# A decoder block on one core: the opening in written order, with half of its first modulation on TensorE, and the later modulation and squares spread over the projection

## The chip, the cores and the metric

The kernel runs on one core of one Trainium2 chip. The metric is the time of one execution in device microseconds (us). Before the change it is 2672.51 us, the median of 3 runs (2671.59 to 2675.07). A core has TensorE (PE, with its weight load PEld), VectorE (DVE), ScalarE (ACT), GpSimd (POOL) and SyncE (SP), which issues the DMA transfers here. Each engine takes its instructions in order and waits on semaphores of the others.

## The reference

One decoder block over 2048 tokens of width 1024, in float32. A condition vector `c` gives six modulation vectors; an RMS norm scaled and shifted by two of them feeds one wide projection, whose columns go to gated linear attention (4 heads) and to dilated attention (8 heads); an output projection, and a second part with up-projection, causal convolution of width 3, SwiGLU and down-projection follow, each added through a gate.

```
cond = silu(c)
mod = cond @ w_ada + b_ada
sh1, sc1, g1, sh2, sc2, g2 = split(mod, 6)
h = rms_norm(x, norm1_g) * (1 + sc1) + sh1
gq, gk, gv, gr, glr, aq, ak, av = split(h @ w_in)
y_gla = gla_group(gq, gk, gv, log_sigmoid(glr @ gla_w_gate + gla_b_gate) / 16, gr, gla_norm_g)
y_att = dilated_attention_group(rms_norm(aq, q_norm_g), rms_norm(ak, k_norm_g), av)
x = x + g1 * (concat(y_gla, y_att) @ w_out)
h = rms_norm(x, norm2_g) * (1 + sc2) + sh2
u_gate, u_val = split(causal_conv(h @ w_up, conv_w, conv_b), 2)
x = x + g2 * ((silu(u_gate) * u_val) @ w_down)
```

## The kernel before

**Tiles.** The tokens are worked in 4 chunks of 512 (`T`), with features on the 128 partitions; a 1024-wide activation is 8 tiles of 128x512, `k` = 0 to 7. Every matrix product is made in three passes (`mm3`, L282–290): weight and activation are each split into a high part and the rest, and high·high, high·low and low·high are summed in PSUM. A weight block of 128x1024 is loaded by SP (`wraw`, 512 KB), its high part is a ScalarE cast (`whi`, L226), its low part a subtraction on VectorE, or on POOL where `pool=True` (`wlo`, L227). `wraw` has 2 buffers, `whi` and `wlo` 3 each. The weights are prepared in the order of `plan` (two blocks ahead of their use).

**Modulation.** `w_ada` is 48 blocks of 128x1024, one for each 128 values of `mod`. `ada(b)` (L317–335) loads a block, multiplies it by `cond` (the condition on every partition) and sums along the row in one VectorE instruction (L330, a reduce), then adds the bias (L331), and for a scale forms `G` (L335). Blocks 0 to 15 (shift and scale of the first norm) are needed first. The other 32, "late" ones, go through a single buffer (`tag="v4"`): a block's load can be issued only when the reduce of the block before is done.

**Opening.** `run` (L941 on) sets up the condition, loads x of the first chunk, forms its mean square (`norm_stats`, L354–371: 8 squares on ScalarE, adds on VectorE, one matmul with `ones`, L367, then Ln and Exp for 1/root), and then for each `k` emits modulation blocks 8+k and k, for k under 4 one of the first four weight blocks of `w_ch` (`FIRST`, low part on POOL), and `norm_mod1` (L373–386): the product with `G` and 1/root on VectorE (L380, "hmul"), the high part on ScalarE (L382), the low part on VectorE (L384, "hlo"). Then the 4 × 8 products of the first blocks stand, and `consts` (L175–204), whose large load waits until the reduce of k = 6 (`GATE`).

**Projection.** `proj(c)` yields steps in the order of `ORDER0` (first chunk) or `ORDER` (L30/31): g and q blocks from `w_ch` (q blocks take an RMS norm of their own, L403–430, with a square whose mean TensorE forms in L411/412, a Newton step over VectorE and POOL, L350–352, and the staged result L420), V blocks (`av`), W blocks (`wide`, four weight parts each accumulated in four PSUM banks; W1 is evacuated in L458–463 by a Tanh on ScalarE and L461 on VectorE). The four chunks' steps are chained, the 32 late modulation blocks are spread over the first 46 steps by `along`, the statistics of the next chunk stand at step 10 of a chunk in one piece, and its `norm_mod` at W1's end. 27 such steps are emitted before mixing of the first chunk starts beside the rest.

**Order.** The program is emitted in this order, and `TC=dict(schedule_with_timeline_sim=True)` hands it to a scheduler, which places the instructions of each engine anew; the engines then run them in the order it chose.

## Time and profile before

| what | us |
|---|---|
| time, median of 3 runs | 2672.51 |
| lowest and highest run | 2671.59, 2675.07 |
| the profiled execution | 2676.88 |
| its span (first to last instruction) | 2675.1 |
| TensorE busy | 2595.0 (granted clock 0.989 of full on the mean) |
| VectorE, ScalarE, POOL busy | 1891.1, 1273.2, 512.1 |

The profile shows one execution. A row of the timeline has its start and its length in us, engine, line, operation, the tile written and those read, and in brackets how long the engine was idle ahead of it and on what it waited. A row of the groups has count, busy time and mean in ns. A row of the waits has the engine and its line, the engine and line that released it, total, times and longest. L-numbers are lines of the kernel before. Some busy shares of the whole, by 40 slices of 67 us, in tenths:

```profile
PE   5988999999989999999999999999999999999999
DVE  8676784665676866777887777778777766666665
POOL 1142451212221311101231111022211110111110
```

TensorE is at nine tenths in all but the first slices.

### The profile page before, as it was taken

The page shows a single profiled execution, that of the slowest core. Times are in us where ns is not written, and L with a number is a line of the kernel's source. Part 1 is how long each engine was busy: PE and PEld are TensorE (multiplying, and loading weights), DVE is VectorE, ACT ScalarE, POOL GpSimd, SP SyncE. Part 2 cuts the span into 40 slices and gives each one's busy share as a digit, 9 for nine tenths or more (in the row PEclk, how much of TensorE's full clock was granted, in tenths as well). Part 3 has the DMA queues.
Part 4 walks back from the last instruction along what each step waited for, and adds up shares of the span by engine and source line. Part 5 has one row for each costly group of instructions (what it writes and reads, how often), then busy time and mean ns, then how long its engine had stood idle before and what let it go on. Part 6 is the DMA issues. An engine that isn't in the chain of part 4 may idle for free.

```text
span 2675.1 us, 46823 instructions
## 1 busy us (share of the span) xinstructions
PE 2595.0 (97%) x18152; PEld 2122.1 (79%) x18152; DVE 1891.1 (71%) x3756; ACT 1273.2 (48%) x2607; POOL 512.1 (19%) x308
## 2 busy tenths in 40 slices
PE   5988999999989999999999999999999999999999
PEld 3777878888768888888788788878888888788887
DVE  8676784665676866777887777778777766666665
ACT  3445556656645455443545444445455443433332
POOL 1142451212221311101231111022211110111110
PEclk9999999999989999999999999999999999999999
DMA  7868455554552244447434444643344445323222
GB/s 276 295 212 276 160 173 170 186 188 150 173 175 95 93 126 133 124 125 241 135 100 135 133 133 129 197 156 122 104 141 138 140 132 180 131 95 101 97 95 95
DMA packets 192127, 405.09 MB, mean 151 GB/s; under 512 B 19473, under 2 KB 70434, under 8 KB 190626
## 3 DMA queue, kind: packets, MB, share of 16 engines
q1 hardware_dynamic: 191906, 402.11, 46.0%
q8 instruction: 143, 2.34, 0.4%
q14 instruction: 78, 0.64, 0.1%
HBM read 339.12 MB, written 62.91 MB: 150 GB/s over the span
## 4 chain that ended last, share of the span: by engine, by line
PE 77%; DVE 5%; ACT 3%; DMA 2%; issue 1%; POOL 0%; SPq 0%; DVEq 0%; ACTq 0%; POOLq 0%
PE psg L288 22%; PE psg L289 22%; PE psg L290 22%; PE psa L719 2%; PE psa L699 2%; PE psa L821 2%; PE psa L557 1%; DVE wlo L227 1%; ACT whi L226 1%; PE psa L816 1%; PE psa L735 1%; ACT big L709 1%; PE psa L627 0%; PE psa L628 0%; DMA sq<-y 0%
## 5 line engine op out<-in xcount | busy, mean ns | idle before, releaser
L288 PE MATMUL psg<-hhi,whi 128*128 128x512 f32 x2040 | 808.7, 399 | 15.6 <-ACT hhi L382 9.0
L289 PE MATMUL psg<-hlo,whi 128*128 128x512 f32 x2040 | 805.6, 395 | 6.4 <-DVE hlo L384 5.0
L290 PE MATMUL psg<-hhi,wlo 128*128 128x512 f32 x2040 | 803.9, 395 | 0.0
L226 ACT CAST whi<-wraw 128x1024 fp32r<-128x1024 f32 (+1 forms) x391 | 409.6, 1049 | 402.5 <-PE psg L289 307.5
L227 DVE TENSOR_TENSOR wlo<-wraw,whi 128x1024 fp32r<-128x1024 f32 (+1 forms) x300 | 386.1, 1287 | 150.2 <-ACT whi L226 141.4
L227 POOL TENSOR_TENSOR wlo<-wraw,whi 128x1024 fp32r<-128x1024 f32 x91 | 223.7, 2459 | 1340.8 <-ACT whi L226 1138.9
L288 PEld LDWEIGHTS psg<-hhi,whi 128*128 128x128 f32 x2040 | 386.2, 190 | 104.8 <-ACT hhi L382 12.3
L289 PEld LDWEIGHTS psg<-hlo,whi 128*128 128x128 f32 x2040 | 386.4, 189 | 90.3 <-DVE hlo L384 9.8
L290 PEld LDWEIGHTS psg<-hhi,wlo 128*128 128x128 f32 x2040 | 386.5, 189 | 82.3 <-issue 2.0
L288 PE MATMUL psg<-ghi,whi 128*128 128x512 f32 x704 | 280.1, 398 | 0.0
L289 PE MATMUL psg<-glo,whi 128*128 128x512 f32 x704 | 277.1, 394 | 0.0
L290 PE MATMUL psg<-ghi,wlo 128*128 128x512 f32 x704 | 276.3, 392 | 0.0
L933 DVE SCALAR_TENSOR_TENSOR x<-psg,mod,x 128x512 f32<-128x512 f32 x192 | 142.7, 747 | 124.4 <-PE psg L290 120.2
L889 DVE SCALAR_TENSOR_TENSOR y<-psg,conv_w_sb,y 128x511 f32<-128x511 f32 x176 | 130.9, 744 | 88.2 <-ACT y L888 87.9
L288 PE MATMUL psg<-whi,hhi 128*128 128x512 f32 (+2 forms) x512 | 177.5, 353 | 10.5 <-DVE stg L461 7.0
L289 PE MATMUL psg<-wlo,hhi 128*128 128x512 f32 (+2 forms) x512 | 178.7, 349 | 7.2 <-DVE wlo L227 7.2
L290 PE MATMUL psg<-whi,hlo 128*128 128x512 f32 (+2 forms) x512 | 177.3, 349 | 0.0
L288 PEld LDWEIGHTS psg<-ghi,whi 128*128 128x128 f32 x704 | 132.5, 188 | 32.2 <-issue 4.5
L290 PEld LDWEIGHTS psg<-ghi,wlo 128*128 128x128 f32 x704 | 132.5, 188 | 28.4 <-issue 1.0
L289 PEld LDWEIGHTS psg<-glo,whi 128*128 128x128 f32 x704 | 132.7, 188 | 28.1 <-issue 2.1
L709 ACT ACTIVATE big<-big,nm 128x256 f32<-128x256 f32 (+1 forms) x256 | 122.4, 479 | 47.1 <-DVE nm L724 47.1
L581 POOL TENSOR_TENSOR pt<-kt,pt 128x512 f32<-128x512 f32 x56 | 92.4, 1650 | 264.2 <-ACT pt L578 186.5
(199 smaller groups left out, 3617.7 us busy)
## 6 DMA issues: line engine op xcount, KB each, us to landing
wraw<-in_w_up_dram SPq DMA_DIRECT2D x176, 512.0 KB, 3.3
wraw<-in_w_down_dram SPq DMA_DIRECT2D x88, 512.0 KB, 3.3
wraw<-in_w_ch_dram SPq DMA_DIRECT2D x48, 512.0 KB, 4.2
wada<-in_w_ada_dram SPq DMA_DIRECT2D x40, 512.0 KB, 5.0
v<-v SPq DMA_DIRECT2D x68, 256.0 KB, 5.1
wraw<-in_w_tokw_dram SPq DMA_DIRECT2D x32, 512.0 KB, 3.9
wraw<-in_w_out_dram SPq DMA_DIRECT2D x32, 512.0 KB, 4.0
sq<-in_xT_dram SPq DMA_DIRECT2D x48, 256.0 KB, 3.9
```

Source lines behind the costliest of these rows:

```text
L226: nc.scalar.copy(hi[:, :n], raw[:, :n])
L227: (nc.gpsimd if pool else nc.vector).tensor_tensor(lo[:, :n], raw[:, :n], hi[:, :n].bitcast(F32), op=ALU.subtract)
L288: nc.tensor.matmul(ps, wh, hh, start=first and k == 0, stop=False, skip_group_check=shared)
L289: nc.tensor.matmul(ps, wh, hl, start=False, stop=False, skip_group_check=shared)
L290: nc.tensor.matmul(ps, wl, hh, start=False, stop=k == n - 1, skip_group_check=shared)
L581: nc.gpsimd.tensor_tensor(kh, gk, df, op=ALU.mult)
L699: nc.tensor.matmul(at(i, hh, z), q[H[hh], i * P:(i + 1) * P], key(H[hh], i, z), start=True, stop=True, skip_group_check=True)
L709: nc.scalar.activation(t[:, lo:hi], t[:, lo:hi], AF.Exp, bias=nm[:, hh, g, i:i + 1], scale=2.0 ** -(h + 1), accum_out=dn[:, hh, g, i:i + 1])
L719: nc.tensor.transpose(ps[:n, i * P:(i + 1) * P], part(S[hh], i), self.C("id"))
L821: nc.tensor.matmul(out, lhsT, rhs, start=first[hh], stop=False, skip_group_check=True)
L889: nc.vector.scalar_tensor_tensor(y[:, 1:], ps[:, :T - 1], self.cw[:, 1, b:b + 1], y[:, 1:], op0=ALU.mult, op1=ALU.add)
L933: nc.vector.scalar_tensor_tensor(x1, ps, self.mod[:, 40 + cb:41 + cb], x1, op0=ALU.mult, op1=ALU.add)
```

## The change

**The opening** is written out in `begin` (called in place of the opening part of `run`), and its instructions on TensorE, VectorE, ScalarE and SP are pinned: `Pinned` hands each to `keep_in_program_order`, so the scheduler leaves their order. In it

- modulation columns k = 0 to 3 (blocks 0 to 3 and 8 to 11) come from a second layout of the same weights, `w_ada1`, in two groups of 2 MB. `ada_rows` multiplies each by the condition on TensorE: 8 products of a 128x32 operand `crep` (the condition's column repeated 32 times) with 128x512 of weights, into four column groups of one PSUM bank, copied by ScalarE; `ada_sum` brings the result to a column with 4 products of one column each, and VectorE adds the bias and forms `G`. Columns 4 to 7 are still reduced on VectorE;
- 36 matmuls of `ones` by `ones` (128x128), whose result isn't read, stand at the head of TensorE's program;
- the low parts of the four first weight blocks are made on VectorE (on POOL before);
- the first four blocks' products stand between the activations in written order, not behind them.

**Later.** The constants' loads all wait for the last early reduce (`GATE` 7), and the four small instructions on them (`const_ops`) stand after 7 steps of the projection. The late modulation (`ada_late`) is loaded and reduced in halves of 128x512 (256 KB), through one buffer of its own (`tag="th"`), 64 halves spread over 91 emitted steps. The statistics of the next chunk (`stats`) make one square in a step, 10 steps spread over a chunk's, in place of one piece at step 10. As before, 27 steps of the projection stand before the mixing.

```diff
-GATE = 6
+GATE = 7
+WARM = 36
...
+    def ada_rows(self, u, raws):
+        ps = self.pa()
+        for k in range(KD):
+            j = k % 4
+            self.nc.tensor.matmul(ps[32 * j:32 * j + 32], self.crep[:, k], raws[k], start=k < 4, stop=k >= 4, skip_group_check=True)
+        t = self.tmp.tile([P, T], F32, name="sq", bufs=3)
+        self.nc.scalar.copy(t, ps)
+        return t
+
+    def ada_sum(self, u, t):
+        nc = self.nc
+        pm = self.pa()
+        for i in range(4):
+            nc.tensor.matmul(pm[:, i:i + 1], t[:, i * P:(i + 1) * P], self.sel, start=True, stop=True, skip_group_check=True)
...
+    def ada_late(self):
+        nc = self.nc
+        for i in (2, 4, 3, 5):
+            for b in range(8 * i, 8 * i + KD):
+                m = self.mod[:, b:b + 1]
+                for j in range(2):
+                    cols = slice(j * T, (j + 1) * T)
+                    raw = self.up.tile([P, T], F32, name="wada", tag="th", bufs=1)
+                    ld = nc.sync.dma_start(raw, self.A["w_ada"][b][:, cols])
+                    if b == 16 and not j:
+                        self.after(ld)
+                    yield
+                    nc.vector.tensor_tensor_reduce(raw, raw, self.cond[:, cols], 0.5, m if j else 0.0, ALU.mult, ALU.add, m)
+                self.ada_end(b)
...
+    def begin(self):
+        plain = self.nc
+        nc = self.nc = PinnedAll(self.tc)
...
+        idle = self.pa()
+        for _ in range(WARM):
+            nc.tensor.matmul(idle[:, 0:P], self.ones, self.ones, start=True, stop=True)
...
+        whi(0)
+        wlo(0)
...
+        t = self.ada_rows(0, rows[0])
+        ms = self.pa()
+        nc.tensor.matmul(ms, self.ones, acc, start=True, stop=True)
...
+        self.ada_sum(0, t)
+        hmul(0)
+        whi(1)
+        hmul(1)
+        hlo(0)
+        wlo(1)
+        hlo(1)
+        whi(2)
+        wlo(2)
+        mm(0, 0, 1)
+        mm(1, 0, 1)
+        mm(2, 0)
+        t = self.ada_rows(1, rows[1])
+        whi(3)
+        next(late[0], None)
+        wlo(3)
+        mm(2, 1)
+        self.ada_sum(1, t)
+        hmul(2)
+        hmul(3)
+        mm(3, 0, 1)
+        hlo(2)
+        hlo(3)
+        for k in (2, 3):
+            for b in FIRST:
+                mm(b, k)
+        for k in range(4, KD):
...
-        def ahead(g, n, c):
-
-            for i, _ in enumerate(g):
-                if i == n:
-                    rstd[c] = self.norm_stats(src(c))
+        def stats(c):
+            acc = None
+            x = src(c)(0)
+            for k in range(KD):
                 yield
...
+                nx = src(c)(k + 1) if k + 1 < KD else None
+                acc = self.square(acc, x, x)
+                x = nx
+            yield
+            rstd[c] = self.norm_end(acc)
+            yield
+
+        def ahead(c, g):
+            return along(stats(c), 10, g, 14)
+
+        first = proj(0)
+        for _ in range(7):
+            next(first)
+        self.const_ops()
+        gemm = along(self.ada_late(), 64, chain(ahead(1, first), ahead(2, proj(1)), ahead(3, proj(2)), proj(3)), 91)
+        for _ in range(20):
             next(gemm)
```

Three places of VectorE's order, of before and of the change apart. A row has the line, the operation, the tile written and those read, and the size; numbers behind names tell tiles apart. `ISA` is a reduce, followed by a short row that reads its sum out.

The first is the opening, from the first multiplication by `G` on. VectorE before:

```order
L380 SCALAR_TENSOR_TENSOR x_164<-x_164,G1_110,rstd_207 128x512
L330 ISA wada_241,mod_109<-wada_241,cond_93,mod_109 128x512
L330 ISA mod_109 128x1
L335 SCALAR_TENSOR_TENSOR G1_110<-mod_109,norm1_g_sb_95 128x1
L331 TENSOR_TENSOR mod_109<-mod_109,b_ada_sb_99 128x1
L380 SCALAR_TENSOR_TENSOR x_166<-x_166,G1_110,rstd_207 128x512
L384 SCALAR_TENSOR_TENSOR hlo_237<-x_164,mod_109,hhi_235 128x512
L330 ISA wada_262,mod_109<-wada_262,cond_93 128x1024
```

VectorE of the change, where pinned instructions all bear the line of the helper, L143:

```order
L143 TENSOR_TENSOR mod_170<-psa_323,b_ada_sb_151 128x2x2
L143 SCALAR_TENSOR_TENSOR G1_171<-mod_170,norm1_g_sb_149 128x2
L143 SCALAR_TENSOR_TENSOR x_173<-x_173,G1_171,rstd_320 128x512
L143 SCALAR_TENSOR_TENSOR x_175<-x_175,G1_171,rstd_320 128x512
L143 SCALAR_TENSOR_TENSOR hlo_333<-x_173,mod_170,hhi_331 128x512
L143 TENSOR_TENSOR wlo_335<-wraw_199,whi_334 128x1024
L143 SCALAR_TENSOR_TENSOR hlo_340<-x_175,mod_170,hhi_338 128x512
L143 TENSOR_TENSOR wlo_345<-wraw_201,whi_344 128x1024
L143 ISA wada_304,mod_170<-wada_304,cond_147 128x1024
```

The two columns' sums come from PSUM (`psa`) at once, the reduces between the two columns are gone, and the low parts of the weight blocks stand among the activations.

The second is the first wide block W0 of the first chunk, between the low parts of its third and fourth weight part (first and last row). VectorE before:

```order
L227 TENSOR_TENSOR wlo_804<-wraw_801,whi_803 128x1024
L330 ISA wada_795,mod_109<-wada_795,cond_93 128x1024
...
L350 SCALAR_TENSOR_TENSOR nwt_726<-psa_720,eps_103,sq_711 128x512
L365 TENSOR_TENSOR rstd_865<-rstd_865,sq_897 128x512
L330 ISA wada_909,mod_109<-wada_909,cond_93 128x1024
...
L330 ISA wada_943,mod_109<-wada_943,cond_93 128x1024
...
L330 ISA wada_989,mod_109<-wada_989,cond_93 128x1024
L330 ISA mod_109 128x1
L227 TENSOR_TENSOR wlo_834<-wraw_831,whi_833 128x1024
```

VectorE of the change:

```order
L260 TENSOR_TENSOR wlo_846<-wraw_843,whi_845 128x1024
...
L416 ISA wada_996,mod_170<-wada_996,cond_147,mod_170 128x512
...
L416 ISA wada_1112,mod_170<-wada_1112,cond_147 128x512
...
L416 ISA wada_1175,mod_170<-wada_1175,cond_147,mod_170 128x512
...
L416 ISA wada_1235,mod_170<-wada_1235,cond_147 128x512
...
L416 ISA wada_1309,mod_170<-wada_1309,cond_147,mod_170 128x512
...
L416 ISA wada_1372,mod_170<-wada_1372,cond_147 128x512
...
L260 TENSOR_TENSOR wlo_884<-wraw_881,whi_883 128x1024
```

Four whole reduces stood between the two weight parts, and six halves stand there now; `const_ops`' four instructions stand there too (left out).

The third is between the staged results (`stg`) of two neighbouring blocks in the first chunk, q4 and q5 (first and last row). VectorE before:

```order
L420 SCALAR_TENSOR_TENSOR stg_1269<-stg_1270,kgs_473,sq_1263 128x512
L331 TENSOR_TENSOR mod_109<-mod_109,b_ada_sb_99 128x1
L227 TENSOR_TENSOR wlo_1482<-wraw_1479,whi_1481 128x1024
L330 ISA wada_1756,mod_109<-wada_1756,cond_93 128x1024
L330 ISA mod_109 128x1
L350 SCALAR_TENSOR_TENSOR nwt_1339<-psa_1334,eps_103,sq_1325 128x512
L331 TENSOR_TENSOR mod_109<-mod_109,b_ada_sb_99 128x1
L352 SCALAR_TENSOR_TENSOR sq_1325<-nwt_1339,sq_1325 128x512
L330 ISA wada_1790,mod_109<-wada_1790,cond_93 128x1024
L330 ISA mod_109 128x1
L420 SCALAR_TENSOR_TENSOR stg_1331<-stg_1332,kgs_473,sq_1325 128x512
```

VectorE of the change:

```order
L512 SCALAR_TENSOR_TENSOR stg_1284<-stg_1285,kgs_532,sq_1278 128x512
L416 ISA wada_2710,mod_170<-wada_2710,cond_147,mod_170 128x512
...
L260 TENSOR_TENSOR wlo_1503<-wraw_1500,whi_1502 128x1024
L416 ISA wada_2774,mod_170<-wada_2774,cond_147 128x512
L416 ISA mod_170 128x1
L432 SCALAR_TENSOR_TENSOR nwt_1356<-psa_1351,eps_155,sq_1342 128x512
L434 SCALAR_TENSOR_TENSOR sq_1342<-nwt_1356,sq_1342 128x512
L416 ISA wada_2895,mod_170<-wada_2895,cond_147,mod_170 128x512
L416 ISA mod_170 128x1
L512 SCALAR_TENSOR_TENSOR stg_1348<-stg_1349,kgs_532,sq_1342 128x512
```

Two whole reduces stood between the two results; three halves stand there now.

More of the change, by code (lines that the diff above doesn't have):

```diff
@@ L129, in chain, with __init__, __getattr__, call @@
         yield from g
+class Pinned:
+    def __init__(self, tc, eng):
+        self.tc, self.eng = tc, eng
+    def __getattr__(self, name):
+        f = getattr(self.eng, name)
+        def call(*a, **kw):
+            r = f(*a, **kw)
+            self.tc.keep_in_program_order(r)
+            return r
+        return call
+class PinnedAll:
+    def __init__(self, tc):
+        for e in ("tensor", "vector", "scalar", "sync"):
+            setattr(self, e, Pinned(tc, getattr(tc.nc, e)))
 class K:
@@ L204, in consts, with const_ops @@
             self.sb.append(t)
+    def const_ops(self):
+        nc = PinnedAll(self.tc)
+        nc.vector.tensor_scalar(self.qgs, self.C("qsc"), self.qg[:, 0:1], -0.5, op0=ALU.mult, op1=ALU.mult)
+        nc.vector.tensor_scalar(self.kgs, self.kg, -0.5, None, op0=ALU.mult)
+        nc.vector.tensor_scalar(self.gB, self.gB, 0.5, None, op0=ALU.mult)
+        nc.vector.tensor_copy(self.blk, self.C("blk"))
     def scratch(self):
@@ L964, in run @@
-        for b in FIRST:
-            for k in range(KD):
-                self.mm3(done[b], ws[b][k:k + 1], h0[k:k + 1], k == 0, True)
+        done, rstd, h0 = self.begin()
         self.consts()
@@ L985, in proj @@
             yield from self.proj(c, hs.pop(), (lambda: begin(c + 1)) if c < 3 else None, () if c else done)
-        def ahead(g, n, c):
-            for i, _ in enumerate(g):
-                if i == n:
-                    rstd[c] = self.norm_stats(src(c))
+        def stats(c):
+            acc = None
+            x = src(c)(0)
+            for k in range(KD):
                 yield
-        gemm = along(chain(*(self.ada(8 * i + k) for i in (2, 4, 3, 5) for k in range(KD))), 32, chain(ahead(proj(0), 10, 1), ahead(proj(1), 10, 2), ahead(proj(2), 10, 3), proj(3)), 46)
-        for _ in range(27):
+                nx = src(c)(k + 1) if k + 1 < KD else None
[12 more added lines that the diff above has]
+        for _ in range(20):
             next(gemm)
```

189 lines of the change are left out of this document (140 added, 49 removed).

## The prediction

> **What bounds the kernel now.** I read first the page's busy times and slices, then the windows cut at the places where TensorE stops, then the waits of TensorE and VectorE, then the timelines around each stop.
>
> ```profile
> span 2675.1 us, 46823 instructions
> PE 2595.0 (97%) x18152; PEld 2122.1 (79%) x18152; DVE 1891.1 (71%) x3756; ACT 1273.2 (48%) x2607; POOL 512.1 (19%) x308
> 0.00:22.00 22.00, 2.08 (x2) 0.51 (x3) 16.18 (x34) 11.51 (x16) 3.07 (x6) 1.00 0.92 340
> 22.00:43.60 21.60, 14.62 (x30) 9.08 (x31) 21.60 (x47) 5.55 (x7) 5.54 (x3) 1.00 0.79 257
> 43.60:61.50 17.90, 15.66 (x69) 12.22 (x67) 13.89 (x27) 4.26 (x7) 1.90 (x1) 1.00 0.58 201
> 61.50:107.00 45.50, 45.06 (x238) 37.97 (x238) 27.75 (x44) 25.86 (x46) 5.30 (x4) 1.00 0.89 312
> 107.00:112.00 5.00, 0.24 (x2) 0.10 (x1) 4.34 (x6) 0.98 (x2) 1.26 (x1) 0.99 0.26 85
> 178.00:215.00 37.00, 26.66 (x240) 20.24 (x239) 33.88 (x48) 20.27 (x34) 21.76 (x18) 0.82 0.66 215
> 215.00:400.00 185.00, 174.71 (x1509) 143.23 (x1508) 136.02 (x193) 100.60 (x185) 69.42 (x46) 0.97 0.59 198
> 400.00:2675.00 2275.00, 2250.86 (x15748) 1843.83 (x15746) 1594.51 (x3299) 1076.17 (x2274) 387.07 (x218) 0.99 0.43 137
> ```
>
> In the windows the columns are length, then busy time (and instructions) of PE, PEld, DVE, ACT, POOL, then granted clock, DMA share, GB/s. TensorE is busy 97% of the span: 80 us of it are idle. 29 of these lie in the first 61.5 us (22.0 − 2.08, 21.6 − 14.62, 17.9 − 15.66), 4.8 in the one stop at 107, 10.3 in 178–215 (where the clock also falls to 0.82) and 10.3 in 215–400. After 400, where the change moves nothing by hand, 24 us are spread over 2275. Each of the early stops has its releaser:
>
> ```profile
> PE psa L367 <- DVE rstd L365: 14.6, 1, 14.6
> PE psg L288 <- ACT hhi L382: 8.6, 3, 5.4
> PE psa L411 <- ACT sqr L405: 4.6, 1, 4.6
> PE psg L288 <- DVE stg L461: 3.9, 1, 3.9
> DVE wada L330 <- DMA wada<-in_w_ada_dram: 25.8, 18, 3.1
> ```
>
> (Total, times, longest.) The last row is VectorE's, over 62–400: there it stands 25.8 us in 18 waits for modulation weights to land, and TensorE's stops are behind that. The profiled execution took 2676.88 us, 4.37 above the median of 2672.51; I sum against it and subtract that.
>
> **A. The opening: −4 (−6.5 to +1).** Of before:
>
> ```profile
> 9.47 2.59 ACT L360 ACTIVATE sq<-x 128x512 f32<-128x512 f32 x4 [0.30 <-DMA x<-in_xT_dram]
> 14.57 2.08 PE L367 MATMUL psa<-rstd,ones 128*128 128x512 f32 x2 [14.57 <-DVE rstd L365]
> 15.29 1.04 ACT L226 CAST whi<-wraw 128x1024 fp32r<-128x1024 f32 x1 [3.23 <-DMA wraw<-in_w_ch_dram]
> 16.60 3.24 DVE L330 CUSTOM_DVE_ANT_0 wada<-wada,cond 128x1024 f32<-128x1024 f32 x1 [0.48 <-DMA wada<-in_w_ada_dram]
> 20.45 0.74 DVE L380 SCALAR_TENSOR_TENSOR x<-x,G,rstd 128x512 f32<-128x512 f32 x1
> 22.00 1.73 PE L288 MATMUL psg<-hhi,whi 128*128 128x512 f32 x2 [5.35 <-ACT hhi L382]
> 28.75 1.22 DVE L330 CUSTOM_DVE_ANT_0 wada<-wada,cond 128x1024 f32<-128x1024 f32 x1
> 37.23 2.33 DVE L331 TENSOR_TENSOR mod<-mod,b_ada_sb 128x1 f32<-128x1 f32 x1
> 57.72 0.74 DVE L384 SCALAR_TENSOR_TENSOR hlo<-x,mod,hhi 128x512 fp32r<-128x512 f32 x1
> 61.47 0.39 PE L288 MATMUL psg<-whi,hhi 128*128 128x272 f32 x1 [0.81 <-ACT stg L437]
> L384 DVE SCALAR_TENSOR_TENSOR hlo<-x,mod,hhi 128x512 fp32r<-128x512 f32 x8 | 5.9, 743 | 0.7 <-ACT hhi L382 0.7
> ```
>
> The eight early columns k set the end, 61.47. Removed: eight of sixteen reduces (about 1.2 each undisturbed, as at 28.75) and POOL's four lo parts (2.4 to 2.6 each, beside which the reduce at 16.60 took 3.24 and a one-column add at 37.23 2.33). Added: sixteen TensorE products with 32 columns, two ACT copies, and the lo parts on VectorE (1.29 each, L227 of the page's groups).
>
> First product. The last x lands near 11.4 (four squares of 0.65 begin at 9.47). The first cast starts at 15.29, the third 512 KB after it: (15.29 − 11.4)/3 = 1.3 us per 512 KB. Five such loads stand ahead of the first group, so they end at 11.4 + 5 × 1.3 = 17.9. The group (its last pair 1 to 2), the mean's matmul (1 to 2), Ln and Exp (1.3 together) bring the first multiplication by G to T = 22.4, against 20.45: the change begins **2 us later**. An estimate with the half-speed spacing of matmuls gives 23.4, with the full-speed one 21.4.
>
> From T on nothing waits for a load. hmul, hi, whi and lo of two columns and three blocks end 6.9 (full speed) to 9.1 us (half) after T on TensorE; the second group, its copy (0.6) and the cast of the fourth block (1.0) start its lo part at T + 10.5 to 13.4, and I take 12.4. It takes 1.2. Then VectorE's fixed row: the sum's two small ones 0.4; hmul and hlo of two columns 2.7; a reduce with its add 1.35; an hmul 0.7; three rounds of two reduces with adds (2.8), hmul and hlo (0.7 each), 4.2 each; a G more and the last hlo behind ScalarE's hi 1.8: 19.6 in all, to T + 33.2. Some 12 matmuls at 0.23 follow. So the wide V0 block starts at 22.4 + 33.2 + 2.7 = 58.3, taken as 58 (55 to 62) against 61.47: −3.5, and −4 with half of the 0.8 idle ahead of that row, which is a ScalarE copy that will have been free longer. The constants' 710 KB, which held VectorE 2.3 us before 57.45, are behind the last reduce and no longer ahead of an hlo. What is late next is VectorE itself: it is the chain from T on.
>
> **B. The first wide block: +3 (0 to +6).** Before:
>
> ```profile
> 89.59 1.23 DVE L227 TENSOR_TENSOR wlo<-wraw,whi 128x1024 fp32r<-128x1024 f32 x1 [0.25 <-DMA sq<-in_xT_dram]
> 92.90 1.23 DVE L330 CUSTOM_DVE_ANT_0 wada<-wada,cond 128x1024 f32<-128x1024 f32 x1 [2.09 <-DMA wada<-in_w_ada_dram]
> 108.93 1.76 DVE L330 CUSTOM_DVE_ANT_0 wada<-wada,cond 128x1024 f32<-128x1024 f32 x1 [0.66 <-DMA wada<-in_w_ada_dram]
> 111.90 0.79 PE L289 MATMUL psg<-wlo,hhi 128*128 128x512 f32 x1 [4.76 <-DVE wlo L227]
> wada<-in_w_ada_dram SPq DMA_DIRECT2D x40, 512.0 KB, 5.0
> sq<-in_xT_dram SPq DMA_DIRECT2D x48, 256.0 KB, 3.9
> ```
>
> One buffer holds the modulation weight, so a reduce, the issue and the landing follow one another: from 92.90 to 108.93 three rounds of 5.3. Between the lo parts of the third and fourth parts of W0 lay four of these; TensorE waited 4.76 for the fourth lo part. The new order has six halves there. No row has a half-size modulation load; the nearest are the 256 KB loads of x (3.9 median) and the 512 KB one (5.0). With SP stuck behind stores as before a half's round can be hardly shorter than a full one's; with free queues it is 2.5. I take 3.6 (a half's reduce 0.7 plus 2.9, a little under the row of 256 KB since the median holds queued loads). Six give 21.6 against 4 × 5.3 = 21.2. The part is thus about as late as before against its block, which now starts 3.5 earlier; with the stats' squares (0.68 adds, one per step) and const_ops' four (1.0) ahead of it the stop grows from 4.8 to about 8.
>
> **C. The q chain: −5 (−8 to 0).**
>
> ```profile
> 167.24 0.74 DVE L420 SCALAR_TENSOR_TENSOR stg<-stg,kgs,sq 128x512 f32<-128x512 f32 x1
> 172.79 2.15 DVE L330 CUSTOM_DVE_ANT_0 wada<-wada,cond 128x1024 f32<-128x1024 f32 x1 [1.49 <-DMA wada<-in_w_ada_dram]
> 178.44 1.22 DVE L330 CUSTOM_DVE_ANT_0 wada<-wada,cond 128x1024 f32<-128x1024 f32 x1 [0.73 <-DMA wada<-in_w_ada_dram]
> 179.59 0.75 DVE L420 SCALAR_TENSOR_TENSOR stg<-stg,kgs,sq 128x512 f32<-128x512 f32 x1
> 183.16 0.50 PE L411 MATMUL psa<-sqr,blk 128*128 128x512 f32 x1 [4.63 <-ACT sqr L405]
> 187.42 0.79 PE L288 MATMUL psg<-whi,hhi 128*128 128x512 f32 x1
> 267.00 0.47 PE L411 MATMUL psa<-sqr,blk 128*128 128x512 f32 x1 [1.17 <-DVE kt L566]
> 268.69 0.65 PE L288 MATMUL psg<-hhi,whi 128*128 128x512 f32 x1
> ```
>
> Stage q4 to stage q5 took 12.35 us because two full reduces with 1.49 and 0.73 of waiting and 2.15 and 1.22 of work stand between. Of the new order three halves stand there: 3 × 0.68 instead of 3.37, and each waits by its own load. 12.35 − 1.3 − (0 to 2.2) gives 9 to 11; I take 9, and TensorE's 4.63 becomes 1.3. With the stop the half-speed stretch behind it goes: matmuls from 187.42 on run 0.43 apart for seven, 1.4 us lost there and about 0.4 in the shorter rows ahead. Together −5.
>
> The trace shows how small a stop suffices: after 1.17 us idle at 267.00 the matmul at 268.69 takes 0.65 instead of 0.39. So a stop cut to 1.3 may keep the clock's 1.8 and C be −3.2, which its range holds. The Trainium skill, TensorE: Matmul & The Clock Gate, HAM oscillation, has it that only idle gaps of more than about 3.4 us bring the throttle back, which would leave C at −5; the 4.63 at 183 agrees with it, the 1.17 at 267 does not.
>
> **D. W1's evacuation: −1.5 (−4 to +3).** TensorE waited 3.89 for `stg` of L461 while the next chunk's hmul, hlo and copies came between VectorE's four; now four of ACT's and four of VectorE's stand together. What came between is not removed, only later; hence the plus.
>
> **E. The second chunk: +1 (−3 to +9).** Before, all 32 late columns are through VectorE after its 30th weight part, 10 of them in the second chunk; now 36 halves lie there. No row shows a half's wait; the nearest is 25.8/18 = 1.4 us per waiting full. VectorE has 185 − 136 = 49 us free in 215–400, about 14 of which lie beside TensorE's own short stops. Thus 36 halves fit while each waits under (49 − 14)/36 ≈ 1 us; their work is 36 × 0.7 = 25 against 10 × 1.33 = 13.
>
> **F. The rest: 0 (±4).** The scheduler places later work anew; nothing in rows of before says which way. The first two chunks' squares on one step each remove a burst, which only D's place shows as waited for.
>
> Sum: −4 + 3 − 5 − 1.5 + 1 + 0 = −6.5, so 2676.9 − 6.5 = 2670.4 for a profiled execution and **2666 us** for the median. Its own range is 2662 to 2671.
>
> **Rivals.**
>
> Wash (0.24): the wide block needs its fourth lo part at a time set by loads, not by when the block starts. Then A comes back whole in B (+4), and C gives half: about 2672 to 2675. For it speaks 92.90 to 108.93, where the spacing was the loads' alone; against it, that the loads too start earlier.
>
> Slower (0.14): the halves choke VectorE in the second chunk. Each holds the in-order VectorE until its 256 KB land, with the weights' lo parts queued behind it. If a half waits as long as a full did, 1.4, 36 × (1.4 − 1.0) = 14 us lie over the cover, and two or three new stops with the clock behind them (1.4 as at 187.42) add 3: E is +17 instead of +1, 2682. It decides from 1.0 us per half on. For it: 18 waits of 31 before. Against: a half is landed 1.3 us earlier where bandwidth sets it (1.3 per 512 KB is 0.65 per half).
>
> Not as it says (0.05): the four groups of 32 columns do not run side by side. The mean's matmul of the same width takes 2.08 for its two instructions (14.57), some 0.85 apart at half speed; sixteen one behind another are 13.6, and started as their loads land they end near 27.6 instead of 19.8: +8 at T, and +5 for the second group at full speed, with 2 of clock: 2681. Against: nothing of the trace, whose narrow products sit in other shapes.
>
> Larger gain (0.15): the 36 idle matmuls keep full speed through the opening. Products at 0.23 apart instead of the 0.43 that the same blocks had between 22 and 43.6 shorten T to 21.4 and the fourth lo part to T + 10.5: −6.5 in A; with C and D at their far ends (−8 and −4) and B at +1 about −15.5, so 2657. For it speaks that the opening's idle stretches are now under 2.5; against it, the row at 267. By the Trainium skill, TensorE: Matmul & The Clock Gate, Part 1: The HAM clock gate, some 3.4 us of activity frees the clock and only an idle window as long loses it, which would be this case; no row here shows the clock held over such a stretch.
>
> **How the numbers follow.** Forecast 0.42, of which 0.28 below 2667.2 and 0.14 above; wash 0.24; slower 0.14 and 0.05; larger gain 0.15. A measurement of this kernel tells 0.2%, 5.3 us, from no change: 2667.2 to 2677.9. Faster: 0.28 + 0.15 = 0.43. Same: 0.14 + 0.24 = 0.38. Slower: 0.19. For 8 in 10 the range takes the larger gain with B at 0 and F at −4 on one side (2652) and the slower case with a little over it on the other (2684).
>
> **What would show it.** A: V0's first 128x272 matmul at 55 to 62, POOL without wlo before it, matmuls 0.23 apart from the start or 0.43. B: the wait of the fourth part's L289-kind matmul near 8. C: q4 to q5 under 11 and no half clock behind it. E: the halves' waits in 200–400 on VectorE, 1 us each or less. Wrong it is if the halves' waits for DMA sum to more than 50 us, if the opening's VectorE waits for TensorE longer than 13 us, or if the later 2275 us move by more than 5.

## The result: 36 us slower, and the profile after

The changed kernel takes 2709.79 us (median of 4, 2708.02 to 2712.34), the kernel before, run beside it, 2673.79: a ratio of 1.0136, 95% interval [1.0121, 1.0151]. That is 36 us more; 2666 was forecast, and 2652 to 2684 for 8 in 10. The page and the windows of the profile after, cut where those of before were cut:

```profile
span 2706.1 us, 47197 instructions
PE 2620.1 (97%) x18272; PEld 2137.1 (79%) x18272; DVE 1884.2 (70%) x3794; ACT 1276.5 (47%) x2611; POOL 500.3 (18%) x304
0.00:22.00 22.00, 16.89 (x98) 12.60 (x98) 10.20 (x20) 11.69 (x17) 0.73 (x5) 1.00 0.90 336
22.00:43.60 21.60, 18.36 (x73) 11.91 (x74) 15.26 (x27) 6.85 (x9) 0.00 (x0) 0.84 0.82 319
61.50:107.00 45.50, 36.95 (x191) 30.56 (x190) 20.36 (x39) 19.88 (x37) 3.79 (x3) 0.94 0.82 280
107.00:112.00 5.00, 5.00 (x13) 3.84 (x13) 2.60 (x6) 2.36 (x3) 1.91 (x2) 0.50 0.47 138
215.00:400.00 185.00, 164.83 (x1356) 133.89 (x1355) 137.66 (x226) 90.93 (x166) 66.92 (x48) 0.91 0.60 199
400.00:2706.00 2306.00, 2274.82 (x15984) 1861.71 (x15982) 1616.67 (x3341) 1089.96 (x2298) 398.35 (x224) 0.99 0.42 138
```

VectorE works no more than before (1884.2 against 1891.1 us). What is new is idle time of TensorE in 61.5–107 (8.5 us, 0.4 before) and in 215–400 (20.2 us, 10.3 before), and a lower clock behind it: 0.50 in 107–112, 0.91 in 215–400 (0.97 before). TensorE's busy time hides this: it grew by 25 us, partly the new products of the opening, partly matmuls at half speed.

Windows compare the same time, not the same work. So I counted in every trace the columns of all products that go to `psg` (4,823,040 in each kernel) and noted when a share of them is through. The second column is the kernel before in us, the others what each kernel is late by (negative: ahead). Each column is one profiled execution; e5 to e12 are experiments told below.

```
share   before   after    e9     e11    e10    e5     e7     e6     e12
 2.5%    97.88   -3.6   +1.3   +4.6   +1.8   -3.6   +0.5   -2.0   -3.4
 3.5%   127.14   +5.0   +2.0   +6.2   +0.9   +5.5   +7.7   -0.4   -5.4
   5%   161.13   +5.0   +2.0   +6.2   +0.9   +5.5   +7.7   -0.4   -5.4
   6%   199.72   +6.9   +2.3  +10.9   +6.9   +7.5   +6.5   +0.9   -1.6
 6.5%   217.21   +5.5   +1.2   +8.8   +5.6   +6.7   +7.7   +1.0   +4.8
   8%   254.39   +7.5   -0.7   +9.8   +8.6   +4.5   +5.6   -1.2   +6.3
   9%   285.01  +14.9   +2.2  +13.6  +14.9   +6.7   +9.3   +3.2  +10.2
  13%   402.94  +31.7  +23.9  +34.0  +11.8   +6.2   +8.8   +2.8  +13.2
  25%   743.74  +29.4  +24.2  +53.5  +12.3   +5.0   +8.4   +2.3  +11.8
 100%  2671.25  +30.6  +26.4  +52.0  +11.9   +3.4   +9.8   +4.9  +11.6
```

The column "after" tells where the time goes: 3.6 us ahead at 98 us, 5 behind at 127, 32 behind at 403, and within 3 us of that in the 2270 us that follow. The two profiled executions lie 31 us apart, not 36, and it is these 31 that the column divides. Two places lose them. The first is the stop near 106 us; rows of VectorE, POOL and TensorE of the change around it, and last the row of VectorE before that makes `blk`:

```profile
92.45 0.22 DVE L143 CAST blk<-consts_sb 128x128 fp32r<-128x128 f32 x1
98.59 0.69 DVE L416 CUSTOM_DVE_ANT_0 wada<-wada,cond 128x512 f32<-128x512 f32 x1 [3.45 <-DMA wada<-in_w_ada_dram]
102.12 0.75 DVE L416 CUSTOM_DVE_ANT_0 wada<-wada,cond,mod 128x512 f32<-128x512 f32 x1 [2.84 <-DMA wada<-in_w_ada_dram]
102.80 0.75 DVE L432 SCALAR_TENSOR_TENSOR nwt<-psa,eps,sq 128x512 f32<-128x512 f32 x1
105.64 1.01 DVE L416 CUSTOM_DVE_ANT_0 wada<-wada,cond 128x512 f32<-128x512 f32 x1 [2.03 <-DMA wada<-in_w_ada_dram]
...
103.62 1.26 POOL L433 TENSOR_TENSOR nwt<-nwt,sq 128x512 f32<-128x512 f32 x1 [17.34 <-DVE mod L397]
104.84 1.26 POOL L498 TENSOR_TENSOR sqr<-sq,sqr 128x512 fp32r<-128x512 f32 x1
...
106.16 0.80 PE L504 MATMUL psa<-sqr,blk 128*128 128x512 f32 x1 [6.61 <-POOL sqr L498]
106.75 0.63 PE L321 MATMUL psg<-whi,hhi 128*128 128x512 f32 x1
...
57.59 0.22 DVE L197 CAST blk<-consts_sb 128x128 fp32r<-128x128 f32 x1
```

Read it from TensorE's rows upwards. TensorE stands 6.61 us for the low part of q1's square, which POOL makes; POOL takes its work in order and has q0's Newton product ahead of it; that waits for VectorE's `nwt`; and VectorE stands 2.84 us for a half's load ahead of `nwt`. The products behind the stop take 0.63 us instead of 0.39. The first row matters too: `blk`, the matrix of the q norm's mean, is made only at 92.45 (57.59 before).

The second place is 215 to 430 us. Over VectorE's waits in 62–400 and TensorE's in 62–430 the same pair, a wait of VectorE for a half and one of TensorE for POOL, leads:

```profile
DVE wada L416 <- DMA wada<-in_w_ada_dram: 66.5, 38, 4.0
PE psa L504 <- POOL sqr L498: 17.8, 5, 6.6
PE psg L321 <- DVE stg L553: 8.4, 2, 6.1
```

VectorE now waits 66.5 us in 38 waits for modulation weights where it waited 25.8 in 18.

### The profile page after: what moved, and what is told of

Read it like the earlier page. It is cut to its first block, busy times and chain, and to the rows that moved or that the text cites. A ratio compares the mean times of both kernels' runs of the same rounds, so it can differ in the third digit from the quotient of the medians.

```text
span 2706.1 us, 47197 instructions
## 1 busy us (share of the span) xinstructions
PE 2620.1 (97%) x18272; PEld 2137.1 (79%) x18272; DVE 1884.2 (70%) x3794; ACT 1276.5 (47%) x2611; POOL 500.3 (18%) x304
## 4 chain that ended last, share of the span: by engine, by line
PE 78%; DMA 8%; DVE 8%; ACT 3%; issue 2%; SPq 0%; POOL 0%; DVEq 0%; ACTq 0%; POOLq 0%
PE psg L321 23%; PE psg L322 22%; PE psg L323 22%; DMA wada<-in_w_ada_dram 4%; PE psa L811 2%; PE psa L791 2%; PE psa L913 2%; DVE wlo L260 1%; DVE wada L416 1%; DMA wraw<-in_w_ch_dram 1%; PE psa L649 1%; DMA sq<-in_xT_dram 1%; ACT whi L259 1%; PE psa L827 1%; PE psa L908 1%
## 5 line engine op out<-in xcount | busy, mean ns | idle before, releaser
L321 PE MATMUL psg<-hhi,whi 128*128 128x512 f32 x2016 | 799.8, 398 | 11.6 <-ACT hhi L474 3.1
L322 PE MATMUL psg<-hlo,whi 128*128 128x512 f32 x2016 | 793.8, 394 | 0.2 <-DVE hlo L476 0.2
L323 PE MATMUL psg<-hhi,wlo 128*128 128x512 f32 x2016 | 793.3, 394 | 0.0
L260 POOL TENSOR_TENSOR wlo<-wraw,whi 128x1024 fp32r<-128x1024 f32 x88 | 217.7, 2474 | 1286.2 <-ACT whi L259 1144.7
L322 PEld LDWEIGHTS psg<-hlo,whi 128*128 128x128 f32 x2016 | 380.9, 189 | 80.8 <-issue 3.8
L323 PEld LDWEIGHTS psg<-hhi,wlo 128*128 128x128 f32 x2016 | 380.8, 189 | 81.0 <-issue 1.9
```

The source lines that it names most:

```text
L260: (nc.gpsimd if pool else nc.vector).tensor_tensor(lo[:, :n], raw[:, :n], hi[:, :n].bitcast(F32), op=ALU.subtract)
L321: nc.tensor.matmul(ps, wh, hh, start=first and k == 0, stop=False, skip_group_check=shared)
L322: nc.tensor.matmul(ps, wh, hl, start=False, stop=False, skip_group_check=shared)
L323: nc.tensor.matmul(ps, wl, hh, start=False, stop=k == n - 1, skip_group_check=shared)
```

## The experiments

Each was timed beside the kernel before, on the same chip as it. Three theories stood: **H**, a reduce that waits for its load holds the in-order VectorE and all behind it, and halves through one buffer double the number of such waits; **P**, what costs is that modulation now lies in the second chunk; **S**, the squares spread one to a step cost something. Later came **C**, the place of the four instructions on the constants, and **W**, an earlier start is lost again to what loads and VectorE set.

| kernel | ratio to before, 95% interval |
|---|---|
| the change | 1.0136 [1.0121, 1.0151] |
| e1 change, late blocks whole as before | 1.0053 [1.0037, 1.0068] |
| e2 change, halves through two buffers | 1.0067 [1.0048, 1.0086] |
| e3 change, squares in one piece | 1.0127 [1.0110, 1.0144] |
| e4 before + halves over 91 steps | 1.0093 [1.0072, 1.0113] |
| e9 before + halves over 46 steps | 1.0098 [1.0082, 1.0114] |
| e10 before + halves over 46 steps, two buffers | 1.0038 [1.0026, 1.0051] |
| e11 before + quarters over 46 steps | 1.0200 [1.0184, 1.0215] |
| e8 before + spread squares | 0.9995 [0.9985, 1.0004] |
| e7 before + late constants | 1.0040 [1.0024, 1.0055] |
| e5 the opening alone (with late constants) | 1.0020 [1.0010, 1.0031] |
| e6 e5, constants sooner | 1.0024 [1.0013, 1.0034] |
| e12 change, whole blocks, constants sooner | 1.0039 [1.0025, 1.0052] |
| e13 e12, first late load ahead | 1.0018 [1.0008, 1.0027] |
| e14 e6, first late load ahead | 1.0015 [1.0005, 1.0025] |
| e15 before, late blocks from step 7 | 0.9994 [0.9984, 1.0004] |

**Whole blocks in the change (e1).**

```diff
-                    raw = self.up.tile([P, T], F32, name="wada", tag="th", bufs=1)
+                raw = self.at.tile([P, 1024], F32, name="wada", tag="v4", bufs=1)
...
-along(self.ada_late(), 64, ... 91)
+along(self.ada_full(), 32, ... 39)
```

> The changed kernel, with the late modulation put back into whole 512 KB blocks through the old buffer, spread so that it ends at the same step as before (32 blocks over 39 steps after the first seven); opening and one-square-per-step statistics stay as changed. Theory H (each half holds the in-order VectorE for a load, and there are twice as many): VectorE's waits for wada in 62-440 fall from 66 us to about 26, the time falls to 2665-2675, with the opening's 3.5 us kept. Rival P (what costs is that modulation lies in the second chunk at all): the same, 2665-2675, since it is gone from there too. Rival S (the squares of the next chunk, one in a step, do the harm): stays at 2700-2712.

Measured: 2688.8 against 2675.1. The waits for `wada` in 62–440 are 34.2 us. So 22 of the 36 us went with the halves; 14 stayed, more than H or P had foreseen, and less than S.

**Two buffers in the change (e2).**

```diff
-raw = self.up.tile([P, T], F32, name="wada", tag="th", bufs=1)
+raw = self.up.tile([P, T], F32, name="wada", tag="th", bufs=2)
```

> The changed kernel, its 64 halves at the same places but through two buffers, so that a load can be issued while the half before is reduced (to make room the condition's column operand and the convolution's constants share other memory). Theory H: VectorE's waits for wada in 62-440 fall from 66 us to under 15 and the time to 2668-2685. Rival P: the halves' work is still in the second chunk, 2700-2712. Rival S: 2700-2712.

Measured: 2692.34 against 2675.1. Some 19 of the 36 us are gone, and S falls for that part, since the squares stay spread. P does not: the halves are emitted where they were, but they do not run there. With two buffers the last is reduced at 266 us (399 in the change), and 11 are reduced after 215 us instead of 35, so this run takes them out of the second chunk as well. The waits fell only to 41.9 us, and the time stayed 7 us above the upper end that H gave. The edit does more than the line shown: the loads of the convolution's constants come later, and the tile `th` of the second part, which shares the tag, gets two buffers too.

**Halves alone (e4) and halves at the old pace (e9).** Both put `ada_late` into the kernel before, e4 over 91 steps as in the change, e9 over 46.

```diff
-along(chain(*(self.ada(8 * i + k) for i in (2, 4, 3, 5) for k in range(KD))), 32, ... 46)
+along(self.ada_late(), 64, ... 46)
```

> The kernel before, with one part of the change: the 32 late blocks as 64 halves of 256 KB through one buffer, spread over 91 steps. Theories H and P: 2700-2715 (the loss of 39 us behind the opening without the opening's gain), VectorE's waits for wada in 62-440 at 60-70 us. Rival S: within 4 us of before.

> The kernel before, with the late modulation in halves through one buffer as in e4, but spread over 46 steps, so that no more of it lies in the second chunk than before. Theory H (the wait for each half is what costs, wherever it stands): VectorE's waits for wada in 62-440 at 60-80 us and a loss of 15 to 35 us, 2690-2710. Rival P (the second chunk is what costs): within 6 us of before.

Measured: 2701.16 against 2675.1 (e4) and 2703.98 against 2677.78 (e9), 26 us each. The pace at which they are emitted changes nothing. This says nothing against P, since it did not change where they run: in e9 they still run until 371 us (383 in e4; the last late reduce before ended at 267), and 18 of them lie behind 285 us (20 in e4, none before). Not the program's spread sets the pace but the round of reduce, issue and landing. Among reduces that had to wait, one begins 5.8 us (median) after the one before it in the kernel before and 4.2 in e9: half the bytes, but twice the rounds.

**Two buffers (e10) and quarters (e11), each beside e9.**

```diff
-raw = self.up.tile([P, T], F32, name="wada", tag="th", bufs=1)
+raw = self.up.tile([P, T], F32, name="wada", tag="th", bufs=2)
```

```diff
-for j in range(2):
-    cols = slice(j * T, (j + 1) * T)
+for j in range(4):
+    cols = slice(j * 256, (j + 1) * 256)
```

> The kernel of e9 (the kernel before with late halves over 46 steps), through two buffers instead of one, all else alike (the convolution's constants share memory with the condition to make room). Theory H: the waits for wada fall from 76 us to 20-40, and the time falls from e9's 2704 to 2675-2688. If the number of reduces is what costs and not their waiting, it stays at 2695-2708.

> The kernel of e9 with the late modulation in 128 quarters of 128 KB through one buffer, over the same 46 steps: the waiting instructions doubled once more, bytes alike. Theory H: a wait of 1 us or more for each, 120-160 us of waits for wada in 62-500, and 2715-2760. If halves cost by their place in the order alone: 2698-2712.

Measured: 2686.83 and 2731.73, against 2674.55. e10 has the same two side effects as e2. VectorE's waits in 62–500 us, of before, e9, e10 and e11 in this order:

```profile
DVE wada L330 <- DMA wada<-in_w_ada_dram: 25.8, 18, 3.1
```

```profile
DVE wada L351 <- DMA wada<-in_w_ada_dram: 75.7, 46, 3.8
```

```profile
DVE wada L356 <- DMA wada<-in_w_ada_dram: 37.6, 30, 4.3
```

```profile
DVE wada L351 <- DMA wada<-in_w_ada_dram: 125.5, 77, 3.9
```

With the same bytes, the time rises with the waits in total: 12 us more of them cost 12 us (e10), 50 more cost 26 (e9), 100 more, and some 20 behind that window, cost 57 (e11). With two buffers the same 64 halves cost less than half, so it is the single buffer that makes halves dear (the side effects of that edit apart, which no run separates). e11's 125.5 is at the lower edge of what was expected, its time inside it.

Where the time is lost is another matter, and there neither H nor P holds alone. Up to 254 us e9 has waited 45.3 us for halves (22.5 before) and is not late at all (−0.7). Between 285 and 403 it waits 21.9 us (none before) and loses 21.7; the change waits 21.7 there and loses 16.8, e4 waits 18.9 and loses 18.4. In the kernels whose late modulation ends by 290 us this stretch costs between −3.1 and +3.2 us. So late in the second chunk about as much is lost as is waited, and up to 254 us the waits cost e9 nothing. One of the late waits in e9, on VectorE and then on TensorE:

```profile
287.12 1.02 DVE L351 CUSTOM_DVE_ANT_0 wada<-wada,cond 128x512 f32<-128x512 f32 x1 [3.10 <-DMA wada<-in_w_ada_dram]
...
289.21 0.48 DVE L586 COPY_PREDICATED kt<-masks_sb,psa 128x128 f32<-128x128 uint32 x2
...
289.55 0.26 PE L577 MATMUL psa<-pt 64*32 64x32 f32 x8 [2.01 <-DVE kt L586]
```

VectorE stands 3.10 us for a half, `kt` comes behind it, and TensorE stands 2.01 us for `kt`. Two buffers both shorten the waits and end the late modulation at 253 us (e10), ahead of this stretch, so no run tells how much of the 26 us is the waiting and how much the place. Nor is it shown why e10 loses 14 us between 161 and 285, where e9 loses nothing.

**Spread squares (e8 and e3).** e8 puts `stats` and its `along(..., 10, ..., 14)` into the kernel before, e3 takes it out of the change; in short:

```diff
-def ahead(g, n, c): ... rstd[c] = self.norm_stats(src(c)) at step n
+def ahead(c, g): return along(stats(c), 10, g, 14)
```

> The kernel before, with the one-square-per-step statistics alone. If its cost is its own: 8 to 10 us as between e1 and e5, 2681-2686. If it needs the opening or the constants' place: within 3 us of before.

> The changed kernel, with the statistics of the next chunk in one piece at the old step; opening, halves and the place of the constants stay. If the spread squares cost 9 us beside the opening, as between e1 and e5: 2698-2703. If they cost nothing of their own, as in e8: 2707-2713.

Measured: 2675.91 against 2677.78 (no difference), and 2711.85, the change's own time. Alone the squares cost nothing, and beside halves nothing that shows. Beside whole blocks in the change they are followed by 9 us (e1 against e5, which differ by them alone), by 5 to 6 (e12 against e6, below) and by none (e13 against e14). They have no price of their own; what makes the difference is open.

**The opening alone (e5).** Halves and squares put back.

> The changed kernel with both later parts put back: whole late blocks through the old buffer, and the statistics of the next chunk in one piece at the old step; what is left of the change is the opening and the place of the constants. H, P and S alike: the opening's gain of 3 to 4 us and nothing else, 2667-2672. If the opening itself sets off the stop at the first wide block, 2674-2682.

Measured: 2680.08 against 2675.1. The opening is 3.6 us ahead at 98 us as in the change, and 5.5 behind at 127:

```profile
104.51 0.79 PE L517 MATMUL psa<-sqr,blk 128*128 128x512 f32 x1 [6.84 <-ACT sqr L511]
```

Here no half is in play. Ahead of q0's mean stood 235 products to `psg` in TensorE's order before, and 282 stand there now; ahead of q1's stood 291, and 294 now. Since `blk` comes late, the scheduler moved q0's mean 47 products back, almost onto q1's. Between the second matmul of q0's mean and the first of q1's lie 12 products now (51 before, from 240 to 291), and no more than these hide q0's chain over ScalarE, VectorE and POOL. The time lies in the range given for such a stop.

**Constants sooner (e6) and constants late (e7).** e6 is e5 with `const_ops` after 5 steps and `blk` ahead of `gB`; e7 is the kernel before with the four instructions pinned after 7 steps.

```diff
         first = proj(0)
-        for _ in range(7):
+        for _ in range(5):
             next(first)
         self.const_ops()
```

> The opening alone (the kernel of e5), with the four small instructions on the constants emitted after 5 steps of the projection instead of 7, the block matrix of the q norm ahead of the group norm's gain. Ahead of the mean of q0 then stand 239 products on TensorE (282 in e5, 235 before). Theory C (the place of these four made q0's norm late and put q1's right behind it): the mean of q0 near 84 us, the stop of 6.8 us near 104 is gone, the time is 2667-2673. Rival W (an earlier start only means a longer wait for what loads and VectorE set): the stop stays in some form and the time at 2677-2682.

> The kernel before, with these four small instructions alone moved: pinned, after 7 steps of the projection, as in the change (287 products then stand ahead of the mean of q0, 235 before). Theory C: a stop of 4 to 8 us ahead of q1's mean near 105 us, and 2678-2685. Rival W: within 3 us of before.

Measured: e7 2686.16 against 2677.78; e6 2683.25 against 2677.78. e7 shows the mechanism in the kernel before: 8 to 11 us for moving four instructions that together last 1 us, with stops of 2.27 and 4.70 at q1's mean. The time is a little above C's range. In e6 the local part came out as C had it:

```profile
85.61 0.50 PE L517 MATMUL psa<-sqr,blk 128*128 128x512 f32 x1
```

q0's mean is at 85.61 (94.34 in e5), the stop at 104 is gone, and 127 us finds the kernel 0.4 ahead instead of 5.5 behind. But the time did not follow: e6 loses 3 to 4 us by 285 and 3 more between 740 and 890 (where e7, e9, e10 and e11 lose as much), ends no better than e5, and lies above the ranges of both C and W.

**The change without both harmful parts (e12).** e1 with the constants of e6.

> The changed kernel without its two harmful parts: late modulation in whole blocks as before, the four small instructions on the constants after 5 steps with the block matrix ahead; the opening and the spread squares stay. If the costs simply add (opening alone with late constants +5, its constants -6 to -9, squares 0): 2667-2676, no worse than before. If the squares cost 9 beside whole blocks, as between e1 and e5: 2679-2686. In either case the stops near 104-107 us should be gone and the first 160 us ahead of before by 1 to 4 us.

Measured: 2687.72 against 2676.72, above both ranges that were given. Only the local part holds, and more than holds: the long stops near 104–107 us are gone, and it is 5.4 us ahead at 161 us, the best of all. Then 15 us go by 285. Around W1's evacuation VectorE has no free moment from 192 to 214, and TensorE waits for it:

```profile
211.18 0.79 PE L321 MATMUL psg<-whi,hhi 128*128 128x512 f32 x1 [8.41 <-DVE stg L567]
```

In 165–215 VectorE is busy 41.7 us in both kernels, with 60 (before) and 63 instructions. Here the lead of TensorE ended where VectorE was the one waited for.

**The late blocks' start (e13, e14, e15).** In e6 and e12 no late block is reduced by 70 us (two before), and the last ends at 282 and 290 (267 before). Theory **L** took this backlog for the cause, **R** the scheduler's new order as a whole.

```diff
         done, rstd, h0 = self.begin()
+        late = self.ada_full()
+        next(late)
         self.consts()
```

> The kernel of e12, with the first late block's load issued ahead of the constants' and the late blocks spread from the fifth step on (31 over 42), so that the late modulation is as far at 110 us as before. Theory L: the lead of the first 160 us is kept, less some 2 us that VectorE waits for that load: 2668-2676. Rival R: 2680-2690 like e12.

> The kernel of e6 (statistics in one piece), with the same earlier start of the late modulation. Theory L: 2668-2676. Rival R: 2678-2687 like e6.

> The kernel before, with the late modulation started after seven steps of the projection and spread over the next 39, so that it ends at the same step. Theory L: the backlog of two to three blocks costs 5 to 10 us, 2680-2686. Rival R: within 3 us of before.

Measured: 2680.72, 2680.49 and 2674.66 against 2675.72. e13 is 6 us better against its runs of before than e12, e14 1 to 2 better than e6, which the intervals do not tell from none; neither reaches what L said, and both lie in R's ranges. But none of the three changed what L blames. In e13 and e14 the first late block is reduced at 57 and 58 us, the second only at 75, and by 110 us they have begun 6 and 7 late reduces (6 in e12 and in e6, 9 before). e15 tells nothing either: the scheduler placed the late reduces as before (two done at 70 us, the last at 269), so the later start never came about. Why the opening's lead is not kept past 160 us stays open between L and R.

## Why the prediction was wrong, point by point

The step that failed most is E, the price of halves in the second chunk; before it comes one that B left out, what the four instructions on the constants release. By the share table the change's 31 us come in this order: A −3.6 up to 98 us, B and the constants +8.6 up to 127, nothing up to 161, C +1.9 up to 200, D −1.4 up to 217, E +26 up to 403, and −1 behind it. The prediction's own sign of being wrong came true: the halves' waits sum to 66.5 us, and it had named 50.

**A, the opening: right, −4 forecast.** The wide V0 block was put at 58 us:

```profile
21.55 1.41 DVE L143 SCALAR_TENSOR_TENSOR x<-x,G,rstd 128x512 f32<-128x512 f32 x2 [0.24 <-ACT rstd L143]
...
23.11 0.51 PE L143 MATMUL psg<-hhi,whi 128*128 128x512 f32 x1 [2.20 <-ACT hhi L143]
24.49 0.63 PE L143 MATMUL psg<-hhi,wlo 128*128 128x512 f32 x1
24.91 0.63 PE L143 MATMUL psg<-hhi,whi 128*128 128x512 f32 x1
57.92 0.28 PE L321 MATMUL psg<-whi,hhi 128*128 128x272 f32 x1
```

It starts at 57.92, 3.55 earlier than before. T is 21.55 instead of 22.4, and the products behind it still run at half speed (24.49 to 24.91), so the larger gain did not come. (Its sum was also off: the terms as listed, with E's +1, give −16.5 and not −15.5.) The groups of 32 columns do run side by side: in the second group four such products start within 0.02 us, at 30.69 to 30.71.

**The constants: not priced, and this is the first step that failed.** In B the four instructions were counted with their duration ("const_ops' four (1.0)"). What they release was left out: `blk` stands ahead of q0's mean. Their place costs 8 to 11 us alone (e7), and with it put right the change is ahead at 127 us instead of 5 behind (e12 against e1). What that is worth in the end is less clear: the time gained 3 us in e12 against e1 and none in e6 against e5. The order on TensorE tells of it before any run, 235 against 283 products ahead of the mean; the working had looked at VectorE's order only.

**B, the first wide block: round right, place and price wrong.** A half's round of 3.6 was forecast; 98.59, 102.12 and 105.64 lie 3.5 apart. The stop of 8 was forecast at W0's fourth lo part; there TensorE waits 1.33:

```profile
115.82 0.50 PE L322 MATMUL psg<-wlo,hhi 128*128 128x512 f32 x1 [1.33 <-DVE wlo L260]
```

The long one, 6.61, is ahead of q1's mean. And the term was +3 where 8.6 us are lost between 98 and 127: two more stops, 1.37 at 99.06 and 2.37 at 123.02, and twelve products at half speed behind the long one were not in it.

**C, the q chain: the gain of 5 did not come.** Of q4 and q5, and of a later stop of TensorE:

```profile
172.67 0.75 DVE L512 SCALAR_TENSOR_TENSOR stg<-stg,kgs,sq 128x512 f32<-128x512 f32 x1
178.73 0.69 DVE L416 CUSTOM_DVE_ANT_0 wada<-wada,cond 128x512 f32<-128x512 f32 x1 [1.96 <-DMA wada<-in_w_ada_dram]
183.86 0.74 DVE L512 SCALAR_TENSOR_TENSOR stg<-stg,kgs,sq 128x512 f32<-128x512 f32 x1
...
182.77 0.51 PE L504 MATMUL psa<-sqr,blk 128*128 128x512 f32 x1 [3.11 <-POOL sqr L498]
...
203.29 0.79 PE L322 MATMUL psg<-wlo,hhi 128*128 128x512 f32 x1 [3.92 <-DVE wlo L260]
```

The link took 11.2 us, the far end of 9 to 11, and the stop is 3.1 (4.63 before) and not 1.3. It is now a wait for POOL. The 1.5 us won there are lost again by 203.29, where the wait for a weight's low part on VectorE is 3.92 (1.48 before).

**E, the second chunk: the step that failed most.** It was priced at +1 with +9 as its end; 26 us are lost from 217 to 403 in the change, 17 of them after 285 (22 in e9). The rival "slower" named this mechanism, halves choking VectorE, and gave it 0.14 and 2682. Its arithmetic failed as well as E's: both treated VectorE's idle time as a store (49 − 14 = 35 us) from which 36 waits of up to 1 us could be paid. In 200–440 the halves wait 26 us, 0.7 each, below that threshold, and the loss is there all the same. What the waits cost went by where they fell, as e9 shows (nothing up to 254 us, 22 us after 285), and not by a sum over the stretch. And E counted 36 halves there without their pace: a round took 4.1 us (median of those that waited, all through the late part), so they reach to 399 us.

**D and F.** W1's evacuation is waited for 2.35 us in the first chunk and 6.07 in the second (3.89 and 2.68 before). So D's −1.5 came in the first chunk; the second lost 3.4, which D had not counted (they are among E's 26). F's ±4 held in the change (−1 behind 403 us), but it is too narrow for such changes: e5 and e1 differ by 9 us through a part that costs nothing alone.

**The row at 267.** The prediction read there that a stop of 1.17 us brings half speed. Between that stop and the slow products lie 64 small products, from 267.64 to 268.7, so the stop alone is not shown to do it.

The parts measured in the kernel before sum to about the whole: halves +26 (e4, e9), late constants +8 to +11 (e7), squares 0 (e8), opening −3.6 up to 98 us, 30 to 33 of the 36. That they add up like this is partly luck, since taken out of the change they do not: whole blocks give back 22 (e1), the constants 0 to 3, and e12, without either, is still 11 us slower than before.

## What to carry to other kernels

A load cut in half is not half a wait: if an in-order engine stands for each piece, count the rounds and not only the bytes. A second buffer took back half of the loss here; whole blocks through one buffer were better still. Idle time of an engine is no store that pays for waits; ask for each wait what stands behind it on that engine, and which engine waits for that. An instruction that lasts 0.2 us can carry a place in the order for others: look what it releases, and compare the order on the engine that is to be kept busy.

## What the runs showed of the hardware

A modulation load of 512 KB lands 4.3 us after its issue (median, 62–400 us, before), one of 256 KB 3.1 to 3.2 through one buffer (the change, e9) and 4.0 through two (e10), one of 128 KB 2.7 (e11). A quarter of the bytes saves 1.6 us, so the rounds shrink far less than the loads.

The clock survives some short stops and not others. In the change the warm-up matmuls stand 0.21 us apart up to 6.3 us and 0.11 from 6.5 on; they end at 11.9. After a stop of 2.38 us the clock is still up, as the matmul pair of the mean shows, which took 2.08 us before:

```profile
19.00 1.13 PE L143 MATMUL psa<-rstd,ones 128*128 128x512 f32 x2
```

Eight products of one column follow, to 20.9, then a stop of 2.20 us, and the products behind that run at half speed until 30 us (granted clock 0.50 in 26–30). Behind a stop of 2.35 us at 213.09 the products went to half speed from 214.9 to 217.9, behind one of 2.37 at 123.02 they did not. So the length of a stop alone does not decide here. The Trainium skill, TensorE: Matmul & The Clock Gate, HAM oscillation, sets the limit near 3.4 us of idleness. None of these stops reached it; with the one-column products counted as idle, the one ahead of 23.1 us comes near, about 3 us.
